# Hybrid decoder trunk: the block levels of a gated recurrence taken two at a time, in matmuls of 192 columns

## Chip, core and metric

One core of a Trainium2 chip runs the whole program. The metric is device time in microseconds (us), the median of three runs. TensorE does the matmuls (PE in the rows, its weight loads PEld), VectorE is DVE, ScalarE is ACT, GpSimd is POOL, and SyncE (SP) issues the transfers.

## What is computed

Two layers of a hybrid block on 256 tokens of width 1024, in f32. A layer is a half-step feed-forward network, a mixer of three branches (latent attention, a gated linear recurrence, attention into a memory), and a second feed-forward network. The change is in the recurrence (4 heads of 128 channels):

```python
def hgrn2_branch(q, f_logit, i_in, gate, lb, o_norm_g):
    qf = silu(q)
    g = logaddexp(log(lb), log1p(-lb) + log_sigmoid(z))     # log of the forget factor f
    k = (1.0 - lb) * sigmoid(-z)
    # S_t = diag(exp(g_t)) S_{t-1} + k_t outer v_t ; o_t = S_t^T q_t
    o = chunk_gated_recurrence(qf, k, v, g)
    return rmsnorm(o, o_norm_g) * silu(gate)
```

Written out, the output at token t is a sum over earlier tokens s of (q_t * f_{s+1} ... f_t) . k_s times v_s. The kernel forms the matrix of these products for each head and for each half of 128 tokens, and the product block of the second half with the first.

## The kernel before

Every large product is a projection: `proj` (weights as the moving operand, 512 columns), `proj_ws` and `proj_wide` (weights stationary). Weights stream from memory in chunks; ScalarE rounds each to `wh`, VectorE writes the rest to `wl` (lines 232 and 233), four buffers of each, and TensorE multiplies in three parts (lines 260 to 262). One sub-chunk is two k-tiles of 512 columns: 12 matmuls. The order of TensorE's and SyncE's work is that of the source. For VectorE and ScalarE a scheduler orders the instructions when the program is built; at run time each engine then goes through its own in that fixed order.

Small steps of the mixer are hung into the projections as jobs, run after the sub-chunk with that number: `{2: [lv(1)]}` runs `lv(1)` after the third. The recurrence uses these.

- `Tf` holds the forget factors, `Qp` and `Kp` (two halves of one tile `QKt`) hold queries and keys, channels on the partitions, tokens along the row, 4 heads of 256 tokens. `AT` collects the products of each half of 128 tokens, `A2` those across the halves.
- `diag` writes the diagonal. Then `level(s)` for s = 1, 2, 4, ..., 64 treats pairs of neighbouring blocks of s tokens: the right block's queries against all 128 keys of the half (8 matmuls of 64 columns, one for each head and half, all into one PSUM bank `hl`). VectorE copies what the mask `mk` allows into `AT` (line 752), then carries the products to the next size: right queries times the left block's factor (line 759), left keys times the right block's (line 760), and the pair's factor (line 762).
- `cross` multiplies the second half's queries with the first half's keys (4 matmuls of 128 columns into `hx`) and ScalarE copies the result to `A2`. `lv(7)` and `lv(8)` both call it.
- The jobs `lv(0)` to `lv(8)` hang in the projections ckv, hi, uk, uqn, hgate (two), gate00 (two) and gate20. Between uqn and hgate stands uqr, the projection whose result feeds the rotary step (`rope_t`, lines 850 to 856), which is VectorE's.
- The PSUM banks of the small steps rotate over four buffers (`aux`), the accumulators of the projections over two (`acc`).

Of the kernel before, what the change touches and what calls it, by code (L numbers as in the profile page):

```python
# [22 lines left out]
NT = SEQ // P  # L23
# [4 lines left out]
HH = 4  # L28
# [5 lines left out]
SK = 2  # L34
LOOKAHEAD = 3
WARM = 9
LEVELS = (1, 2, 4, 8, 16, 32)

SPLITS = (Q_LORA, KV_LORA, ROPE, 512, 512, 512, 512, 512, 3 * D)
OFF = [0]  # L40
# [104 lines left out]
def hybrid_kernel(ctx: ExitStack, tc: tile.TileContext, x, xt, mem, memt, positions, stream, smalls, ident_in, consts,  # L145
                  masks, fnorm, out):
    nc = tc.nc
# [14 lines left out]
    def T4(shape, dtype, name):  # L162
        return t4.tile(shape, dtype, tag="t4", name=name)
# [444 lines left out]
    nc.sync.dma_start(out=ident, in_=ident_in)  # L608


    mk = const.tile([P, len(LEVELS) * 64 + P], mybir.dt.uint8, name="mk")
    pos_i = const.tile([P, NT], I32, name="pos_i")
    memT = const.tile([P, KT, SEQ], F32, name="memT")
    causal = const.tile([P, P], F32, name="causal")
# [5 lines left out]
    sin2 = const.tile([P, NT, ROPE], F32, name="sin2")  # L620

    def setup_rest():
        mraw = T4([P, len(LEVELS) * 64 + P], I32, "mraw")
        nc.sync.dma_start(out=mraw, in_=masks)
        nc.vector.tensor_copy(out=mk, in_=mraw)
        nc.sync.dma_start(out=pos_i, in_=positions)
        nc.sync.dma_start(out=causal, in_=consts)
        nc.gpsimd.memset(AT, 0.0)
        raw = sm[:, LB_OFF:LB_OFF + DEPTH * HH].rearrange("p (l h) -> p l h", l=DEPTH)
        m = tiny.tile([P, HH], F32, tag="lbm", name="lbm")  # L630
        e = tiny.tile([P, DEPTH, HH], F32, tag="lbe", name="lbe")
# [57 lines left out]
    def mixer(l, u, nxt):  # L689
# [5 lines left out]


        QKt = T8([P, 2, HH, SEQ], F32, "QKt")
        Qp, Kp = QKt[:, 0], QKt[:, 1]
        Tf = T4([P, HH, SEQ], F32, "Tf")

        hf_acc = proj_ws(l, "hf", u.xb, {0: [lambda: u.bank(4)], 1: [lambda: u.bank(6)], 2: [u.finish]})
# [21 lines left out]
        def diag():  # L723
            for t in range(NT):
                b = ms_bank("hd")
                for h in range(HH):
                    nc.tensor.matmul(b[:, h * P:(h + 1) * P], lhsT=Kp[:, h, tsl[t]], rhs=Qp[:, h, tsl[t]],
                                     start=True, stop=True)
                m = mk[:, len(LEVELS) * 64:].unsqueeze(1).to_broadcast([P, HH, P])
                nc.vector.copy_predicated(out=AT[:, t], mask=m, data=b.rearrange("p (h c) -> p h c", h=HH))  # L730
            nc.vector.tensor_tensor(out=Qp, in0=Qp, in1=Tf, op=ALU.mult)

        def level(s):
            b = ms_bank("hl")
            nb = P // (2 * s)
            rows = 64 if s == 64 else P
            for t in range(NT):
                for h in range(HH):
                    i = t * HH + h
                    rhs = Qp[:, h, tsl[t]].rearrange("p (n a s) -> p n a s", a=2, s=s)[:, :, 1, :]  # L740
                    nc.tensor.matmul(b[0:rows, i * 64:(i + 1) * 64], lhsT=Kp[:, h, t * P:t * P + rows], rhs=rhs,  # L741
                                     start=True, stop=True)
            if s == 64:
                nc.vector.tensor_copy(
                    out=AT.rearrange("p t h c -> p (t h) c")[0:64, :, 64:P],
                    in_=b[0:64, :].rearrange("p (i c) -> p i c", i=NT * HH))
            else:
                i = LEVELS.index(s)
                m = mk[:, i * 64:(i + 1) * 64].rearrange("p (n s) -> p n s", s=s)
                m = m.unsqueeze(1).to_broadcast([P, NT * HH, nb, s])  # L750
                o = AT.rearrange("p t h (n a s) -> p (t h) n a s", a=2, s=s)[:, :, :, 1, :]
                nc.vector.copy_predicated(out=o, mask=m, data=b.rearrange("p (i n s) -> p i n s", i=NT * HH, s=s))
            q = Qp.rearrange("p h (n a s) -> p (h n) a s", a=2, s=s)
            k = Kp.rearrange("p h (n a s) -> p (h n) a s", a=2, s=s)
            f = Tf.rearrange("p h (n a s) -> p (h n) a s", a=2, s=s)
            n = HH * SEQ // (2 * s)
            tl = f[:, :, 0, 0:1].to_broadcast([P, n, s])
            tr = f[:, :, 1, 0:1].to_broadcast([P, n, s])
            nc.vector.tensor_tensor(out=q[:, :, 1, :], in0=q[:, :, 1, :], in1=tl, op=ALU.mult)
            nc.vector.tensor_tensor(out=k[:, :, 0, :], in0=k[:, :, 0, :], in1=tr, op=ALU.mult)  # L760
            if s < 64:
                nc.vector.tensor_tensor(out=f[:, :, 0, 0:1], in0=f[:, :, 0, 0:1], in1=f[:, :, 1, 0:1], op=ALU.mult)

        def cross():
            b = ms_bank("hx")
# [2 lines left out]
            nc.scalar.copy(out=A2, in_=b.rearrange("p (h c) -> p h c", h=HH))  # L768

        def lv(i):  # L770
            if i < len(LEVELS):
                return lambda: level(LEVELS[i])
            return (lambda: level(64)) if i == len(LEVELS) else cross


        accs = proj_u("cq", {3: [diag]})
# [252 lines left out]
        def gate(b, h, jobs=None):  # L1029
            accs = proj_u(f"gate{b}{h}", jobs)  # L1030
            g = T4([P, NT, 512], F32, f"gate{b}")
            for t in range(NT):
                nc.scalar.activation(out=g[:, t, :], in_=accs[t], func=AF.Copy if h == 0 else AF.Sigmoid,
                                     scale=u.r[:, t:t + 1])
            gts[(b, h)] = g
# [37 lines left out]
        for t in range(NT):  # L1073
            nc.scalar.activation(out=hg["gate"][:, t, :], in_=accs[t], func=AF.Silu, scale=u.r[:, t:t + 1])
        gate(0, 0, {0: [qk_T(ksb, kT, 1), lv(6)], 1: [qk_T(qsb, qT, 1)], 2: [att(0), lv(7)], 3: [att(1)]})
        gate(2, 0, {0: [att(2), lv(8)], 1: [ptr(0)], 2: [ptr(1), att(3)], 3: [app(0)]})
        gate(1, 0, {0: [app(1), ptr(2), att(4)], 1: [ptr(3), hg_out], 2: [app(2), att(5)], 3: [app(3), ptr(4)]})
        mem_T("qmT", "mq", u.xb, [{3: [open_gates, mem_split], 7: [app(4), ptr(5)]}, {3: [hg_T], 7: [app(5)]}])
        mem_T("kmT", "mk", mem_xb, [{}, {}])
# [67 lines left out]
def _consts():  # L1147
    q, k = np.meshgrid(np.arange(P), np.arange(P), indexing="ij")
    c = np.where(k > q, np.float32(NEG), np.float32(0.0)).astype(np.float32)
    m = np.zeros((P, len(LEVELS) * 64 + P), np.int32)  # L1150
    s = np.arange(P)
    for i, h in enumerate(LEVELS):
        t = np.array([t for t in range(P) if (t // h) % 2 == 1])
        m[:, i * 64:(i + 1) * 64] = ((s[:, None] // (2 * h)) == (t[None, :] // (2 * h))) & \
            (((s[:, None] // h) % 2) == 0)
    m[:, len(LEVELS) * 64:] = np.eye(P, dtype=np.int32)
    return c, m


# [26 lines left out]
```

## Time and profile before

| | |
|---|---|
| median of 3 runs | 1304.21 us (1304.02 to 1305.16) |
| the profiled execution's own time | 1304.3 us, its span 1302.5 us |
| mean granted TensorE clock | 0.997 of full speed |
| TensorE busy | 1290.9 us, 99% of the span |
| VectorE busy | 920.4 us, 71% |
| ScalarE busy | 734.3 us, 56% |

The span is the time between the first and the last instruction; the program's time has 1.8 us more around it. Busy times are averages over the whole program. An engine's queue is strictly in order, so a busy share tells nothing of where one of its results comes too late for another engine; that is read from the order and the starts of the instructions. Both layers run the same mixer, the second 642.7 us after the first.

### The profile page before, as it was taken

The page shows a single profiled execution, that of the slowest core. Times are in us where ns is not written, and L with a number is a line of the kernel's source. Part 1 is how long each engine was busy: PE and PEld are TensorE (multiplying, and loading weights), DVE is VectorE, ACT ScalarE, POOL GpSimd, SP SyncE. Part 2 cuts the span into 40 slices and gives each one's busy share as a digit, 9 for nine tenths or more (in the row PEclk, how much of TensorE's full clock was granted, in tenths as well). Part 3 has the DMA queues.
Part 4 walks back from the last instruction along what each step waited for, and adds up shares of the span by engine and source line. Part 5 has one row for each costly group of instructions (what it writes and reads, how often), then busy time and mean ns, then how long its engine had stood idle before and what let it go on. Part 6 is the DMA issues. An engine that isn't in the chain of part 4 may idle for free.

```text
span 1302.5 us, 18358 instructions
## 1 busy us (share of the span) xinstructions
PE 1290.9 (99%) x7139; PEld 1118.1 (86%) x7139; DVE 920.4 (71%) x1433; ACT 734.3 (56%) x1139; POOL 4.6 (0%) x18
## 2 busy tenths in 40 slices
PE   9999999999999999999999999999999999999997
PEld 7888889888888898888898888898888888988885
DVE  6987557777876677775577775577688756777753
ACT  6765446547765465554455554465477644655542
POOL 1000000000000000000000000000000000000000
PEclk9999999999999999999999999999999999999998
DMA  8755554433444545555545555445334455555561
GB/s 292 281 187 191 196 192 150 166 133 128 155 168 162 194 164 192 194 193 180 194 177 194 194 183 189 173 154 171 126 130 162 162 183 176 190 184 183 188 220 51
DMA packets 35801, 231.28 MB, mean 178 GB/s; under 512 B 4225, under 2 KB 4609, under 8 KB 10369
## 3 DMA queue, kind: packets, MB, share of 16 engines
q1 hardware_dynamic: 35568, 230.05, 50.7%
q8 instruction: 56, 0.92, 0.3%
q14 instruction: 33, 0.26, 0.1%
q10 hardware_dynamic: 144, 0.05, 0.0%
HBM read 229.04 MB, written 1.05 MB: 177 GB/s over the span
## 4 chain that ended last, share of the span: by engine, by line
PE 99%; DVE 0%; DMA 0%; ACT 0%; SPq 0%; issue 0%
PE acc L321 26%; PE acc L260 15%; PE acc L262 15%; PE acc L261 15%; PE acc L326 13%; PE hl L741 2%; PE acc L305 2%; PE acc L303 2%; PE acc L301 2%; PE sc L884 1%; PE pt L587 1%; PE nt L404 1%; PE po L901 1%; PE at L587 1%; PE mo L901 0%; PE msc L970 0%
## 5 line engine op out<-in xcount | busy, mean ns | idle before, releaser
L233 DVE TENSOR_TENSOR wl<-raw,wh 128x1024 fp32r<-128x1024 f32 (+2 forms) x435 | 523.6, 1205 | 290.4 <-ACT wh L232 282.9
L232 ACT CAST wh<-raw 128x1024 fp32r<-128x1024 f32 (+2 forms) x435 | 449.3, 1034 | 428.9 <-PE acc L261 271.0
L321 PE MATMUL acc<-nT,wh 128*128 128x512 f32 x1408 | 443.7, 397 | 0.0
L326 PEld LDWEIGHTS acc<-nT,wl 128*128 128x128 f32 x1408 | 264.8, 188 | 62.1
L326 PE MATMUL acc<-nT,wl 128*128 128x256 f32 x1408 | 277.0, 278 | 0.0
L321 PEld LDWEIGHTS acc<-nT,wh 128*128 128x128 f32 x1408 | 214.4, 189 | 0.0
L260 PE MATMUL acc<-wh,hTh 128*128 128x512 f32 x352 | 137.8, 391 | 0.0
L262 PE MATMUL acc<-wl,hTh 128*128 128x512 f32 x352 | 137.3, 390 | 0.0
L261 PE MATMUL acc<-wh,hTl 128*128 128x512 f32 x352 | 137.2, 390 | 0.0
L260 PE MATMUL acc<-wh,nT 128*128 128x512 f32 (+2 forms) x320 | 125.0, 391 | 0.0
L262 PE MATMUL acc<-wl,nT 128*128 128x512 f32 (+2 forms) x320 | 120.5, 377 | 0.0
L261 PE MATMUL acc<-wh,nT 128*128 128x512 f32 (+2 forms) x320 | 120.2, 376 | 0.0
L374 ACT CAST hTh<-jn 128x256 fp32r<-128x256 f32 x80 | 32.4, 406 | 94.9 <-DVE jn L484 94.9
L262 PEld LDWEIGHTS acc<-wl,hTh 128*128 128x128 f32 x352 | 66.1, 188 | 13.8
L260 PEld LDWEIGHTS acc<-wh,hTh 128*128 128x128 f32 x352 | 66.1, 188 | 13.4
L261 PEld LDWEIGHTS acc<-wh,hTl 128*128 128x128 f32 x352 | 66.2, 188 | 13.4
L262 PEld LDWEIGHTS acc<-wl,nT 128*128 128x128 f32 x320 | 60.1, 188 | 10.6
L260 PEld LDWEIGHTS acc<-wh,nT 128*128 128x128 f32 x320 | 60.3, 188 | 8.9 <-ACT qsb L841 0.3
L261 PEld LDWEIGHTS acc<-wh,nT 128*128 128x128 f32 x320 | 60.4, 189 | 8.6
L336 DVE TENSOR_TENSOR jn<-acc,jn 128x512 f32<-128x512 f32 x92 | 62.9, 683 | 0.2
L375 DVE TENSOR_TENSOR hTl<-jn,hTh 128x256 fp32r<-128x256 f32 x80 | 33.9, 424 | 33.6 <-ACT hTh L374 33.6
L301 PE MATMUL acc<-nT,wh 128*128 128x256 f32 x192 | 55.6, 289 | 0.2 <-ACT wh L232 0.2
(295 smaller groups left out, 1583.9 us busy)
## 6 DMA issues: line engine op xcount, KB each, us to landing
raw<-in_stream SPq DMA_DIRECT2D x197, 1024.0 KB, 4.8
raw<-in_stream SPq DMA_DIRECT2D x17, 512.0 KB, 3.6
raw<-in_stream SPq DMA_DIRECT2D x6, 768.0 KB, 4.4
raw<-in_stream SPq DMA_DIRECT2D x4, 576.0 KB, 3.7
x<-in_x SPq DMA_DIRECT2D x4, 256.0 KB, 6.0
memT<-in_memt SPq DMA_DIRECT2D x1, 1024.0 KB, 7.1
mrow<-in_mem SPq DMA_DIRECT2D x2, 512.0 KB, 9.1
out_x<-xg SPq DMA_DIRECT2D x4, 256.0 KB, 2.4
```

The source lines that it names most:

```text
L232: last_wh[0] = nc.scalar.copy(out=wh, in_=raw[:, a:a + m, :])
L233: nc.vector.tensor_tensor(out=wl, in0=raw[:, a:a + m, :], in1=wh.bitcast(F32), op=ALU.subtract)
L260: nc.tensor.matmul(o, lhsT=xh(k)[:, ts], rhs=wh[:, j, :], start=(k == 0), stop=False)
L261: nc.tensor.matmul(o, lhsT=xl(k)[:, ts], rhs=wh[:, j, :], start=False, stop=False)
L262: nc.tensor.matmul(o, lhsT=xh(k)[:, ts], rhs=wl[:, j, :], start=False, stop=(k == nkt - 1))
L301: nc.tensor.matmul(o, lhsT=wh[:, j, fs], rhs=x[:, 0, :], start=first, stop=False, skip_group_check=True)
L303: nc.tensor.matmul(o, lhsT=wh[:, j, fs], rhs=x[:, 1, :], start=False, stop=False, skip_group_check=True)
L321: nc.tensor.matmul(a2[:, f].rearrange("p a c -> p (a c)"), lhsT=wh[:, j, fs], rhs=x.rearrange("p a c -> p (a c)"), start=(k == 0), stop=False,
L326: nc.tensor.matmul(a2[:, f, 0, :], lhsT=wl[:, j, fs], rhs=x[:, 0, :], start=False, stop=(k == KT - 1), skip_group_check=True)
L336: last_join[1] = nc.vector.tensor_tensor(out=s, in0=a2[:, :, 0, :], in1=s, op=ALU.add)
L374: nc.scalar.copy(out=oh, in_=ps)
L375: nc.vector.tensor_tensor(out=ol, in0=ps, in1=oh.bitcast(F32), op=ALU.subtract)
```

## The change

Levels are taken in pairs: `four(i, t)` treats groups of four neighbouring blocks of s = 1, 4 or 16 tokens, for half t. Each group of four holds the pairs of two levels, and what was a level of its own (a block against the one before, two before and three before) comes from one matmul of 192 columns: 96 from `Qp` (blocks 1 to 3) and 96 from a second copy `Qs`, in which blocks 2 and 3 carry one factor more and block 3 two more. `Qs` takes the place of `Kp` in the tile `QKt`; `Kp` gets its own tile. A call makes 4 matmuls into two banks, and six masked copies of 192, 128 and 64 elements. `Qs` is made on VectorE in the call for t = 0; queries, keys and factors are carried on in the call for t = 1. There are six calls, and they stand in the slots of the six levels from 1 to 32. Level 64 stays as it was, and the second `cross` is gone. The mask input grows from 512 to 704 columns.

```diff
-LEVELS = (1, 2, 4, 8, 16, 32)
+LEVELS = (1, 4, 16)
+MCOLS = len(LEVELS) * 192
...
-        Qp, Kp = QKt[:, 0], QKt[:, 1]
+        Qp, Qs = QKt[:, 0], QKt[:, 1]
+        Kp = T4([P, HH, SEQ], F32, "Kp")
...
-        def level(s):
+        def four(i, t):
+            s = LEVELS[i]
+            hn = HH * SEQ // (4 * s)
+            q, z, k, f = (a.rearrange("p h (n b s) -> p (h n) b s", b=4, s=s) for a in (Qp, Qs, Kp, Tf))
+
+            def fb(a, n=1, to=None):
+                return f[:, :, a:a + n, 0:1].to_broadcast([P, hn, to or n, s])
+
+            if t == 0:
+                nc.vector.tensor_tensor(out=z[:, :, 1:3, :], in0=q[:, :, 2:4, :], in1=fb(1, 2), op=ALU.mult)
+                nc.vector.tensor_tensor(out=z[:, :, 3:4, :], in0=z[:, :, 2:3, :], in1=fb(1), op=ALU.mult)
+            for h0 in (0, 2):
+                b = ms_bank("hl")
+                for h in (h0, h0 + 1):
+                    rhs = QKt[:, :, h, tsl[t]].rearrange("p a (n c) -> p a n c", c=4 * s)[:, :, :, s:4 * s]
+                    nc.tensor.matmul(b[:, (h - h0) * 192:(h - h0 + 1) * 192], lhsT=Kp[:, h, tsl[t]], rhs=rhs,
+                                     start=True, stop=True)
+                d = b[:, 0:384].rearrange("p (h a n c) -> p h a n c", h=2, a=2, c=3 * s)
+                o = AT[:, t, h0:h0 + 2].rearrange("p h (n c) -> p h n c", c=4 * s)
+                m0 = i * 192
+                for a, lo, hi in ((0, s, 4 * s), (1, 2 * s, 4 * s), (2, 3 * s, 4 * s)):
+                    w = hi - lo
+                    nq = w * P // (4 * s)
+                    m = mk[:, m0:m0 + nq].rearrange("p (n c) -> p n c", c=w)
+                    m0 += nq
+                    src = d[:, :, 0] if a == 0 else d[:, :, 1, :, 0:w] if a == 1 else d[:, :, 1, :, 2 * s:3 * s]
+                    nc.vector.copy_predicated(out=o[:, :, :, lo:hi],
+                                              mask=m.unsqueeze(1).to_broadcast([P, 2, P // (4 * s), w]), data=src)
+            if t == 1:
+                nc.vector.tensor_tensor(out=q[:, :, 1:2, :], in0=q[:, :, 1:2, :], in1=fb(0), op=ALU.mult)
+                nc.vector.tensor_tensor(out=q[:, :, 2:4, :], in0=z[:, :, 1:4:2, :], in1=fb(0, 1, 2), op=ALU.mult)
+                for a in (2, 1):
+                    nc.vector.tensor_tensor(out=f[:, :, a, 0:1], in0=f[:, :, a, 0:1], in1=f[:, :, a + 1, 0:1],
+                                            op=ALU.mult)
+                nc.vector.tensor_tensor(out=k[:, :, 0:3, :], in0=k[:, :, 0:3, :], in1=fb(1, 3), op=ALU.mult)
+                nc.vector.tensor_tensor(out=f[:, :, 0, 0:1], in0=f[:, :, 0, 0:1], in1=f[:, :, 1, 0:1], op=ALU.mult)
...
-            if i < len(LEVELS):
-                return lambda: level(LEVELS[i])
-            return (lambda: level(64)) if i == len(LEVELS) else cross
+            if i < 2 * len(LEVELS):
+                return lambda: four(i // 2, i % 2)
+            return level64 if i == 2 * len(LEVELS) else cross
...
-        gate(2, 0, {0: [att(2), lv(8)], 1: [ptr(0)], 2: [ptr(1), att(3)], 3: [app(0)]})
+        gate(2, 0, {0: [att(2)], 1: [ptr(0)], 2: [ptr(1), att(3)], 3: [app(0)]})
```

How the built order changes, at the two places of which the prediction speaks. The first is VectorE around the third group (s = 16). Before, after the copy and the carries of the level of 8 tokens (the 752 to 762 rows), come the weight remainders and the rotary step; the next level's matmuls need only what stands in the first four rows.

```order
L752 COPY_PREDICATED AT<-mk,hl 128x64x8
L759 TENSOR_TENSOR QKt<-QKt,Tf 128x64x8
L760 TENSOR_TENSOR QKt<-QKt,Tf 128x64x8
L762 TENSOR_TENSOR Tf<-Tf 128x64
L233 TENSOR_TENSOR wl<-raw,wh 128x1024 x2
L850 TENSOR_TENSOR rope_t<-rope_t,cos_166 128x288
L853 TENSOR_TENSOR rope_t<-rope_t,sin_167 128x9x16 x2
...
L856 COPY ksb<-rope_t 128x8x32
L853 TENSOR_TENSOR rope_t<-rope_t,sin_167 128x9x16
L233 TENSOR_TENSOR wl<-raw,wh 128x1024
L854 TENSOR_TENSOR qsb<-rope_t 128x8x32
```

Now (one line further down in the source, so 234 for 233 and 876 to 882 for the rotary step) the carries of the second group are 764 to 770, and the two products that make the third group's `Qs`, lines 744 and 745, stand behind the rotary step. They are written into `QKt`.

```order
L764 TENSOR_TENSOR QKt<-QKt,Tf 128x64x4
...
L769 TENSOR_TENSOR Kp<-Kp,Tf 128x64x12
L770 TENSOR_TENSOR Tf<-Tf 128x64
L234 TENSOR_TENSOR wl<-raw,wh 128x1024 x2
L876 TENSOR_TENSOR rope_t<-rope_t,cos_166 128x288
L879 TENSOR_TENSOR rope_t<-rope_t,sin_167 128x9x16 x2
...
L234 TENSOR_TENSOR wl<-raw,wh 128x1024
L880 TENSOR_TENSOR qsb<-rope_t 128x8x32
L881 TENSOR_TENSOR rope_t<-rope_t 128x32
L744 TENSOR_TENSOR QKt<-QKt,Tf 128x16x32
L882 COPY ksb<-rope_t 128x8x32
L745 TENSOR_TENSOR QKt<-QKt,Tf 128x16x16
```

What moved: the operands of the next matmuls are no longer complete before the rotary step but after it. The first of the four 192-column matmuls of `four(2, 0)` waits for line 745.

The second place is VectorE between the call for the first group's second half and the second group, a stretch that had two masked copies and six products and now reads:

```order
L761 COPY_PREDICATED AT<-mk,hl 128x64x3
L234 TENSOR_TENSOR wl<-raw,wh 128x1024
L761 COPY_PREDICATED AT<-mk,hl 128x64x2
L761 COPY_PREDICATED AT<-mk,hl 128x64x3
L761 COPY_PREDICATED AT<-mk,hl 128x64
L761 COPY_PREDICATED AT<-mk,hl 128x64x2
...
L765 TENSOR_TENSOR QKt<-QKt,Tf 128x256x2
L769 TENSOR_TENSOR Kp<-Kp,Tf 128x256x3
L770 TENSOR_TENSOR Tf<-Tf 128x256
L234 TENSOR_TENSOR wl<-raw,wh 128x512
L744 TENSOR_TENSOR QKt<-QKt,Tf 128x64x8
L745 TENSOR_TENSOR QKt<-QKt,Tf 128x64x4
```

What moved: carries for four blocks and the new `Qs` all stand between two calls that follow each other on TensorE. TensorE's own order is unchanged but for the calls themselves; the call for the third group stands after hgate's first sub-chunk, where the level of 16 tokens stood:

```order
L261 MATMUL acc<-wh,nT 128x512
L262 MATMUL acc<-wh,nT 128x512
L263 MATMUL acc<-wl,nT 128x512
L750 MATMUL hl<-QKt,Kp 128x192 x4
L261 MATMUL acc<-wh,nT 128x512
```

What moved: eight matmuls of 64 columns became four of 192 in the same place.

## Rows read from the trace of the kernel before

**Rows 1.** The page's busy times by engine.

```profile
PE 1290.9 (99%) x7139; PEld 1118.1 (86%) x7139; DVE 920.4 (71%) x1433; ACT 734.3 (56%) x1139; POOL 4.6 (0%) x18
```

**Rows 2.** Waits of TensorE, the longest: releaser, us in total, times, longest.

```profile
PE warm L198 <- DVE eps_t L546: 1.2, 1, 1.2
```

**Rows 3.** Timeline of TensorE, first layer: start us, us, form; x16 are 8 matmuls.

```profile
247.20 0.48 PE L260 MATMUL acc<-wh,nT 128*128 128x512 f32 x1
...
252.77 1.89 PE L741 MATMUL hl<-QKt 128*128 128x64 f32 x16
...
260.01 1.89 PE L741 MATMUL hl<-QKt 128*128 128x64 f32 x16
261.71 0.48 PE L260 MATMUL acc<-wh,cqT 128*128 128x512 f32 x1
...
263.19 0.28 PE L260 MATMUL acc<-wh,cqT 128*128 128x256 f32 x1
...
265.46 0.50 PE L260 MATMUL acc<-wh,nT 128*128 128x512 f32 x1
...
268.34 1.89 PE L741 MATMUL hl<-QKt 128*128 128x64 f32 x16
...
301.40 1.03 PE L884 MATMUL sc<-kT,qT 96*128 96x256 f32 x4
302.27 1.06 PE L767 MATMUL hx<-QKt 128*128 128x128 f32 x8
303.08 0.47 PE L260 MATMUL acc<-wh,nT 128*128 128x512 f32 x1
```

**Rows 4.** Timeline of VectorE, first layer, levels of 2 and 4 tokens.

```profile
247.83 1.31 DVE L752 COPY_PREDICATED AT<-mk,hl 128x512 f32<-128x512 uint8 x1
248.93 0.22 DVE L348 TENSOR_TENSOR lr_a<-lr_y 128x4 f32<-128x4 f32 x1
...
250.32 0.64 DVE L762 TENSOR_TENSOR Tf<-Tf 128x256 f32<-128x256 f32 x1
250.87 0.68 DVE L233 TENSOR_TENSOR wl<-raw,wh 128x512 fp32r<-128x512 f32 x1
...
254.70 0.71 DVE L752 COPY_PREDICATED AT<-mk,hl 128x512 f32<-128x512 uint8 x1
255.31 0.68 DVE L759 TENSOR_TENSOR QKt<-QKt,Tf 128x512 f32<-128x512 f32 x1
```

**Rows 5.** Timeline of VectorE from the level of 8 tokens to that of 16.

```profile
262.26 0.74 DVE L370 SCALAR_TENSOR_TENSOR vml<-acc,lr_y,vml 128x512 fp32r<-128x512 f32 x1
262.92 0.71 DVE L752 COPY_PREDICATED AT<-mk,hl 128x512 f32<-128x512 uint8 x1
...
264.90 1.22 DVE L233 TENSOR_TENSOR wl<-raw,wh 128x1024 fp32r<-128x1024 f32 x1
...
267.69 0.45 DVE L850 TENSOR_TENSOR rope_t<-rope_t,cos 128x288 f32<-128x288 f32 x1
...
269.95 1.21 DVE L233 TENSOR_TENSOR wl<-raw,wh 128x1024 fp32r<-128x1024 f32 x1
271.08 0.41 DVE L854 TENSOR_TENSOR qsb<-rope_t 128x256 f32<-128x256 f32 x1
...
271.52 0.71 DVE L752 COPY_PREDICATED AT<-mk,hl 128x512 f32<-128x512 uint8 x1
```

**Rows 6.** Windows at the end; after the DVE, ACT and POOL sums come PEclk, DMA share, GB/s.

```profile
1293.00:1294.00 1.00, 0.40 (x2) 0.00 (x0) 0.56 (x1) 0.00 (x0) 0.00 (x0) 1.00 0.00 0
1295.00:1296.00 1.00, 0.00 (x0) 0.00 (x0) 1.00 (x3) 0.88 (x3) 0.00 (x0) 0.74 0.02 8
1296.00:1297.00 1.00, 0.00 (x0) 0.00 (x0) 0.93 (x10) 0.43 (x2) 0.00 (x0) 0.50 0.00 0
```

**Rows 7.** Timeline of TensorE at the start.

```profile
1.19 4.02 PE L198 MATMUL warm<-wz 128*128 128x512 bf16 x9 [1.19 <-DVE eps_t L546]
...
7.41 1.47 PE L198 MATMUL warm<-wz 128*128 128x512 bf16 x6
```

More of the change, by code (lines that the diff above doesn't have):

```diff
@@ L608, in hybrid_kernel @@
     nc.sync.dma_start(out=ident, in_=ident_in)
-    mk = const.tile([P, len(LEVELS) * 64 + P], mybir.dt.uint8, name="mk")
+    mk = const.tile([P, MCOLS + P], mybir.dt.uint8, name="mk")
     pos_i = const.tile([P, NT], I32, name="pos_i")
@@ L622, in setup_rest @@
     def setup_rest():
-        mraw = T4([P, len(LEVELS) * 64 + P], I32, "mraw")
+        mraw = T4([P, MCOLS + P], I32, "mraw")
         nc.sync.dma_start(out=mraw, in_=masks)
@@ L728, in diag @@
                                      start=True, stop=True)
-                m = mk[:, len(LEVELS) * 64:].unsqueeze(1).to_broadcast([P, HH, P])
+                m = mk[:, MCOLS:].unsqueeze(1).to_broadcast([P, HH, P])
                 nc.vector.copy_predicated(out=AT[:, t], mask=m, data=b.rearrange("p (h c) -> p h c", h=HH))
             nc.vector.tensor_tensor(out=Qp, in0=Qp, in1=Tf, op=ALU.mult)
-        def level(s):
+        def four(i, t):
[32 more added lines that the diff above has]
+                nc.vector.tensor_tensor(out=f[:, :, 0, 0:1], in0=f[:, :, 0, 0:1], in1=f[:, :, 1, 0:1], op=ALU.mult)
@@ L734, in level, with level64 @@
+        def level64():
             b = ms_bank("hl")
-            nb = P // (2 * s)
-            rows = 64 if s == 64 else P
             for t in range(NT):
@@ L739, in level @@
                     i = t * HH + h
-                    rhs = Qp[:, h, tsl[t]].rearrange("p (n a s) -> p n a s", a=2, s=s)[:, :, 1, :]
-                    nc.tensor.matmul(b[0:rows, i * 64:(i + 1) * 64], lhsT=Kp[:, h, t * P:t * P + rows], rhs=rhs,
+                    rhs = Qp[:, h, t * P + 64:(t + 1) * P]
+                    nc.tensor.matmul(b[0:64, i * 64:(i + 1) * 64], lhsT=Kp[:, h, t * P:t * P + 64], rhs=rhs,
                                      start=True, stop=True)
[L743 to L758, printed above, removed]
+            nc.vector.tensor_copy(
+                out=AT.rearrange("p t h c -> p (t h) c")[0:64, :, 64:P],
+                in_=b[0:64, :].rearrange("p (i c) -> p i c", i=NT * HH))
+            q, k, f = (a.rearrange("p h (n a s) -> p (h n) a s", a=2, s=64) for a in (Qp, Kp, Tf))
+            n = HH * NT
+            tl = f[:, :, 0, 0:1].to_broadcast([P, n, 64])
+            tr = f[:, :, 1, 0:1].to_broadcast([P, n, 64])
             nc.vector.tensor_tensor(out=q[:, :, 1, :], in0=q[:, :, 1, :], in1=tl, op=ALU.mult)
             nc.vector.tensor_tensor(out=k[:, :, 0, :], in0=k[:, :, 0, :], in1=tr, op=ALU.mult)
-            if s < 64:
-                nc.vector.tensor_tensor(out=f[:, :, 0, 0:1], in0=f[:, :, 0, 0:1], in1=f[:, :, 1, 0:1], op=ALU.mult)
         def cross():
@@ L1149, in _consts @@
     c = np.where(k > q, np.float32(NEG), np.float32(0.0)).astype(np.float32)
-    m = np.zeros((P, len(LEVELS) * 64 + P), np.int32)
+    m = np.zeros((P, MCOLS + P), np.int32)
     s = np.arange(P)
[L1152 to L1156, printed above, removed]
+    c0 = 0
+    for h in LEVELS:
+        b = (s // h) % 4
+        for gap in (1, 2, 3):
+            t = s[b >= gap]
+            m[:, c0:c0 + t.size] = ((s[:, None] // (4 * h)) == (t[None, :] // (4 * h))) & (b[:, None] == b[None, t] - gap)
+            c0 += t.size
+    m[:, MCOLS:] = np.eye(P, dtype=np.int32)
     return c, m
```

## The prediction

> **What bounds the kernel now.** I read the page's busy times first. TensorE is busy for 1290.9 of 1302.5 us [rows 1], so with a granted clock near full the time is the sum of TensorE's work plus whatever makes it wait. The list of TensorE's waits comes next: the longest in the whole program is 1.2 us, at the start [rows 2]. Nothing in the mixers makes TensorE wait, and two things follow. Every matmul taken away shortens the program by its own length, in either layer. And every microsecond by which a new order makes TensorE wait for VectorE or ScalarE lengthens it at full price, since there is no idle time to soak it up. VectorE is busy 71% on the mean [rows 1]; that tells nothing of whether one of its results comes too late, so the third view is the timeline of TensorE beside that of VectorE in the stretch of the recurrence, 245 to 304 us in the first layer [rows 3 to 5]. The second layer is the same stretch 642.7 us later, and the built order of the change is the same in both, so everything below is worked out once and doubled.
>
> **What the change takes off TensorE.** One level of 64-column matmuls goes from 260.01 to 261.71, which is 1.70 us for 16 instructions (each f32 matmul is issued as two), so 106 ns each [rows 3]. Four instructions of 256 columns, the `sc` row at 301.40, take 0.87 us to the next start at 302.27, so 217 ns each [rows 3]. A 256-column instruction costs two 64-column ones and not four, so at 64 columns the columns are not what sets the pace. By columns from the 256-column row, 192 columns cost 217 x 192/256 = 163 ns. A call has 4 matmuls, 8 instructions: 1.30 us in place of 1.70. Six calls: -2.4 us for each layer. The second `cross` ran from 302.27 to 303.08: -0.8 us [rows 3]. Together -3.2 us for each layer, -6.4 in all. Its copy on ScalarE goes too, which TensorE never waited for.
>
> What could spoil this is the way `rhs` is read: for s = 1 three of every four elements, in two pieces. Nothing in the trace shows such a read at 192 columns. The bounds: 163 ns, or, if the 106 ns of the 64-column row were all the reading of its 64 strided columns, 106 x 3 = 318 ns, and a call would be 2.5 us. I take 163, because the 64-column rows are alike for all strides, 1.89 us at each level [rows 3], which points to a cost outside the read.
>
> **What the change adds on VectorE.** Durations here are from start to next start, since instructions overlap by about 0.1 us. A masked copy of 512 elements takes 0.61 us at blocks of 4 tokens (254.70 to 255.31) but 1.10 at blocks of 2 (247.83 to 248.93); a product of 256 elements that lie four apart takes 0.55 (250.32 to 250.87) [rows 4], and a product of 512 elements takes 0.6. With about 0.07 us of fixed cost this is 1 ns an element at runs of 4 or more, and twice that for copies in short runs and for products of lone elements. So the three copies of one bank (192, 128, 64 elements) cost 0.27 + 0.20 + 0.14 = 0.61 us at s = 4 and 16 and 0.47 + 0.34 + 0.20 = 1.01 at s = 1; both banks twice that. `Qs` costs 0.60 + 0.33 (0.62 + 0.55 at s = 1), the carries of queries 0.33 + 0.60 (0.55 + 0.62), of keys 0.87 (768 elements), a factor 0.2 (0.55). For runs of 3 and 2 there is one rule to weigh. The copies in pairs cost double in the row above. The Trainium skill, SBUF — State Buffer, under the section on the DMA port swizzle, says that two or more accesses to a 16-byte line run at full rate; by it the first group's copies would cost 0.61 a bank and the first of the waits below would be 0.8 us shorter. The row contradicts it for these copies, so I go by the row.
>
> This work is off TensorE's path so long as its results come in time. Weight remainders have room: the one written at 250.87 is first used when the second sub-chunk of uqn starts, 261.71 [rows 4, 3]. The results that have little room are `Qs`, keys and queries for the next call. So I follow VectorE's queue from call to call, in the built order.
>
> **Second group, s = 4.** Let T be the start of `four(0, 1)` on TensorE. The next call is due after 1.30 us for the call and 5.57 us of projection (247.20 to 252.77 [rows 3]): T + 6.9. VectorE can begin at T + 0.7, when the first bank is done, and has to get through: one copy 0.47, a remainder 1.14 (269.95 to 271.08 [rows 5]), the other five copies 1.55, queries 1.17, keys 0.87, factor 0.55, a remainder of 512 columns 0.6, `Qs` 0.60 + 0.33. That is 7.3, so T + 8.0, and 0.1 for the hand-over. TensorE waits 1.2 us; if only the 3-element runs go at full rate, 0.8. I take 1.0.
>
> **Third group, s = 16.** Let T be the start of `four(1, 1)`. TensorE's work until the next call: the call 1.30, the rest of uqn 1.48 (261.71 to 263.19), uqr 2.27 (to 265.46), hgate's first sub-chunk 2.88 (to 268.34) [rows 3]. VectorE from T + 0.7: one copy 0.27, a remainder 1.14, `vml` 0.66 (262.26 to 262.92 [rows 5]). uqr needs the accumulator that `vml` frees, so it starts at T + 2.95 and not at 2.78: a wait of 0.2. The next call is therefore due at T + 8.1. VectorE goes on: the last copies and carries 2.93 (0.20 + 0.27 + 0.14 + 0.20 + 0.33 + 0.14 + 0.60 + 0.87 + 0.18), two remainders 2.28, the rotary step 2.26 (267.69 to 269.95), a remainder 1.13, the end of the first rotary half 0.44 (271.08 to 271.52) [rows 5], and only now `Qs`: 0.60, a copy of keys 0.20, 0.33. That reaches T + 13.0, with the hand-over T + 13.1. TensorE waits 5.0 us. Before, the same queue reached 271.52 as late as T + 11.5 counted from the level at 260.01, and nobody noticed: the level at 268.34 needed only what was written before the remainder at 264.90, T + 4.9 [rows 5]. The change puts the operands on the other side of the rotary step. What is queued behind the waiting matmul is the rest of hgate, so everything after it shifts, and none of it is given back. Past this point VectorE has caught up: the next calls need nothing that it has not some microseconds for.
>
> **The clock.** TensorE would stand idle for 5 us. In this trace it was idle as long only once, at the end: its last matmul ends at about 1293.4, and the granted clock is 1.00 until 1295, 0.74 in the next microsecond and 0.50, the lower of its two levels, from 1296 [rows 6]. So after some 2 us of idleness it fell. What it costs to come back the start shows: 9 matmuls of 512 columns take 4.02 us from rest, 447 ns each, while a little later 6 take 1.47, 245 each [rows 7]; the loss is 4.02 - 9 x 0.245 = 1.8 us. For a wait of 5 us the cost is between 0 and 1.8 us; I take 1.5, near the start's, since the wait is more than twice what it took to fall.
>
> **The sum.** For each layer -2.4 - 0.8 + 1.0 + 0.2 + 5.0 + 1.5 = +4.5 us, in all +9.0. The larger mask adds 0.2 us of VectorE's time in the first feed-forward network, under TensorE's projections. The profiled execution took 1304.3 us (1302.5 of span), the median of the runs is 0.1 less: 1313.
>
> **Rivals.**
> Stalls without the clock. The long wait may be shorter than the clock needs: +3.0 a layer, 1310.3. For it, waits under 1 us at the start cost nothing of the kind; against it, the end.
> Faster. VectorE's lag is smaller than I make it, and the third group's `Qs` is there in time. All of the gain then stands: 1304.3 - 6.4 = 1297.9. The place is the wait for line 745 before the third group; with the 1.2 us of the other waits it decides at 2.0 us: shorter, and the change gains. For it, VectorE is 71% busy [rows 1]. Against it, from T + 0.7 on the queue has no gap in my sum, and its pieces are rows of this very stretch; they would have to be 3 us too long in 12.
> Strided reads. If 192 strided columns cost 318 ns, each call costs 1.2 us more: +7.2 a layer, 1327; at s = 1 alone 1318. Against it, that stride makes no difference at 64 columns.
>
> **How the numbers follow.** Waits and clock: 0.50. Waits alone: 0.30. Faster: 0.11. Strided reads: 0.06. The remaining 0.03 is a long wait near its point of decision, no change. One measurement of this kernel tells 0.2%, 2.6 us, from no change. The waits' bounds (4.4 to 5.6 for the long one, 0.8 to 1.3, the clock 0 to 1.8) give +1.9 to +5.9 a layer, 1308 to 1316; the range goes a little beyond, 1306 to 1317, and leaves out the faster case and the strided one. Slower 0.86, same 0.03, faster 0.11.
>
> **What would show it.** A row of waits of TensorE's line 750 for VectorE's line 745, four times in all, near 1 us and near 5 us; uqr waiting some 0.2 us; a granted clock of 0.50 in the microseconds after the longer ones; rows of the calls at 1.3 us, alike for s = 1, 4 and 16. Wrong would be: no wait on line 745, or one under 2 us at the third group, or calls of 2.5 us.

## The result, and the profile after

The changed kernel takes 1316.52 us, the median of 5 runs (1314.95 to 1316.81), against 1304.23 us (1304.02 to 1305.16) for the kernel before: a ratio of 1.0088, with an interval from 1.0077 to 1.0099. It is slower by 12.3 us. The profiled execution took 1315.39 us, with a span of 1313.6 us, 11.1 us longer than the span before; the other four spans lie between 1313.2 and 1315.0. Its mean granted clock is 0.993, before 0.997.

The page's busy times come first; they answer to [rows 1].

```profile
PE 1289.0 (98%) x7027; PEld 1113.7 (85%) x7027; DVE 932.6 (71%) x1505; ACT 733.6 (56%) x1137; POOL 4.6 (0%) x18
```

TensorE has 112 instructions fewer and is busy for 1.9 us less, not the 6.4 us less that the removed matmuls were to give, while the span is 11.1 us longer. So the new time is idle (13.0 us more), and some work also became slower. The list of TensorE's waits (what waits, on what; us in total, times, longest) says where the idle time is. The longest wait of before was the one on `eps_t` [rows 2].

```profile
PE hl L750 <- DVE QKt L745: 12.7, 4, 5.0
PE warm L199 <- DVE eps_t L547: 1.2, 1, 1.2
PE acc L306 <- DVE wl L234: 1.0, 2, 0.6
PE acc L261 <- DVE vml L371: 0.4, 2, 0.2
```

The waits for `eps_t` and for `wl` stand at the program's start, and the kernel before has them too (1.2 us each). All of the new waits but 0.4 us are for one line, the second product of `Qs`. The timeline of TensorE shows them in the first layer, in brackets at the end of a row: before the second group 1.33 us, at uqr 0.22, before the third group 4.99. It answers to [rows 3].

```profile
244.81 1.46 PE L750 MATMUL hl<-QKt,Kp 128*128 128x192 f32 x8
...
253.06 1.54 PE L750 MATMUL hl<-QKt,Kp 128*128 128x192 f32 x8 [1.33 <-DVE QKt L745]
...
259.91 1.46 PE L750 MATMUL hl<-QKt,Kp 128*128 128x192 f32 x8
261.07 0.53 PE L261 MATMUL acc<-wh,cqT 128*128 128x512 f32 x1
...
262.96 0.39 PE L261 MATMUL acc<-wh,cqT 128*128 128x256 f32 x1 [0.22 <-DVE vml L371]
...
273.12 2.93 PE L750 MATMUL hl<-QKt,Kp 128*128 128x192 f32 x8 [4.99 <-DVE QKt L745]
275.60 0.88 PE L261 MATMUL acc<-wh,nT 128*128 128x512 f32 x1
...
278.26 0.40 PE L261 MATMUL acc<-wh,nT 128*128 128x512 f32 x1
...
283.24 1.47 PE L750 MATMUL hl<-QKt,Kp 128*128 128x192 f32 x8
284.41 0.52 PE L261 MATMUL acc<-wh,nT 128*128 128x512 f32 x1
...
285.93 0.40 PE L261 MATMUL acc<-wh,nT 128*128 128x512 f32 x1
```

The call at 273.12 needs 2.48 us to the next start (275.60); the same call at 283.24 needs 1.17. The call and the six matmuls behind it take 5.14 us (273.12 to 278.26) after the long wait and 2.69 (283.24 to 285.93) without it: 2.45 us lost to the clock, besides the wait. The windows show the clock itself (the columns are those of [rows 6]).

```profile
268.00:270.00 2.00, 0.13 (x1) 0.00 (x0) 2.00 (x9) 1.03 (x1) 0.00 (x0) 1.00 0.29 57
270.00:272.00 2.00, 0.00 (x0) 0.00 (x0) 2.00 (x6) 0.00 (x0) 0.00 (x0) 0.81 1.03 430
272.00:274.00 2.00, 0.88 (x3) 0.88 (x4) 1.35 (x5) 0.00 (x0) 0.00 (x0) 0.50 0.09 37
...
276.00:278.00 2.00, 2.00 (x7) 1.54 (x6) 0.90 (x3) 0.00 (x0) 0.00 (x0) 0.50 0.00 0
278.00:280.00 2.00, 2.00 (x10) 1.66 (x9) 0.00 (x0) 0.38 (x1) 0.00 (x0) 0.98 0.00 0
```

TensorE falls idle at 268.13. A mean of 0.81 over the second window is 1.24 us at 1.00 and the rest at 0.50, so the clock fell to the lower of its two levels at about 271.2, 3.1 us into the wait. It is back at 278.1, 5.0 us after TensorE resumed. VectorE is busy all through the first four microseconds (the third sum in a row, 2.00 of 2.00): it is not waiting for anything itself, it is doing other work first. Its timeline says which; it answers to [rows 4, 5].

```profile
245.87 0.44 DVE L761 COPY_PREDICATED AT<-mk,hl 128x192 f32<-128x192 uint8 x1
246.17 1.21 DVE L234 TENSOR_TENSOR wl<-raw,wh 128x1024 fp32r<-128x1024 f32 x1
247.29 1.31 DVE L761 COPY_PREDICATED AT<-mk,hl 128x128 f32<-128x128 uint8 x4
248.39 0.66 DVE L764 TENSOR_TENSOR QKt<-QKt,Tf 128x256 f32<-128x256 f32 x1
248.90 0.45 DVE L761 COPY_PREDICATED AT<-mk,hl 128x64 f32<-128x64 uint8 x1
249.03 0.84 DVE L765 TENSOR_TENSOR QKt<-QKt,Tf 128x512 f32<-128x512 f32 x1
...
252.49 0.42 DVE L745 TENSOR_TENSOR QKt<-QKt,Tf 128x256 f32<-128x256 f32 x1
...
265.75 2.36 DVE L234 TENSOR_TENSOR wl<-raw,wh 128x1024 fp32r<-128x1024 f32 x2
268.02 0.46 DVE L876 TENSOR_TENSOR rope_t<-rope_t,cos 128x288 f32<-128x288 f32 x1
...
270.27 1.22 DVE L234 TENSOR_TENSOR wl<-raw,wh 128x1024 fp32r<-128x1024 f32 x1
271.40 0.42 DVE L880 TENSOR_TENSOR qsb<-rope_t 128x256 f32<-128x256 f32 x1
...
271.84 0.69 DVE L744 TENSOR_TENSOR QKt<-QKt,Tf 128x512 f32<-128x512 f32 x1
...
272.65 0.42 DVE L745 TENSOR_TENSOR QKt<-QKt,Tf 128x256 f32<-128x256 f32 x1
...
285.16 1.28 DVE L761 COPY_PREDICATED AT<-mk,hl 128x192 f32<-128x192 uint8 x6
286.35 0.42 DVE L764 TENSOR_TENSOR QKt<-QKt,Tf 128x256 f32<-128x256 f32 x1
```

From 265.75 to 271.84 VectorE makes weight remainders and the rotary step, and then the two products that TensorE has been waiting for since 268.13. The last two rows are the six copies of the third group's second half, for comparison further down. The second layer repeats this: waits of 1.34, 0.22 and 4.99 us, and a clock that falls 3.4 us after TensorE's last matmul and comes back 5.2 us after it resumes.

### The profile page after: what moved, and what is told of

Same layout as the page of the kernel before. It is cut to its first block, busy times and chain, and to the rows that moved or that the text cites. A ratio compares the mean times of both kernels' runs of the same rounds, so it can differ in the third digit from the quotient of the medians.

```text
span 1313.6 us, 18211 instructions
## 1 busy us (share of the span) xinstructions
PE 1289.0 (98%) x7027; PEld 1113.7 (85%) x7027; DVE 932.6 (71%) x1505; ACT 733.6 (56%) x1137; POOL 4.6 (0%) x18
## 4 chain that ended last, share of the span: by engine, by line
PE 95%; DVE 3%; DMA 0%; issue 0%; ACT 0%; SPq 0%; DVEq 0%
PE acc L322 26%; PE acc L261 15%; PE acc L262 14%; PE acc L263 14%; PE acc L327 13%; PE acc L306 2%; PE acc L304 2%; PE acc L302 2%; DVE wl L234 1%; PE hl L750 1%; PE sc L910 1%; PE pt L588 1%; PE nt L405 1%; PE po L927 1%; PE at L588 1%; DMA xT<-in_xt 0%
## 5 line engine op out<-in xcount | busy, mean ns | idle before, releaser
L327 PE MATMUL acc<-nT,wl 128*128 128x256 f32 x1408 | 276.7, 278 | 0.0
L306 PE MATMUL acc<-nT,wl 128*128 128x256 f32 x192 | 54.7, 285 | 1.1 <-DVE wl L234 1.0
```

What stands on the lines that cost most here:

```text
L306: nc.tensor.matmul(o, lhsT=wl[:, j, fs], rhs=x[:, 0, :], start=False, stop=(k == nkt - 1), skip_group_check=True)
L327: nc.tensor.matmul(a2[:, f, 0, :], lhsT=wl[:, j, fs], rhs=x[:, 0, :], start=False, stop=(k == KT - 1), skip_group_check=True)
```

## The experiments

The theory behind the prediction, called ORDER below: `Qs` of the next group is made too late because of where it stands in VectorE's queue, and the long idle time lets the clock fall. Its rival, LOAD: VectorE simply has too much work in this stretch, with the longer masked copies and carries, and TensorE would wait wherever `Qs` stands. The first four kernels share their runs of the kernel before (median 1304.34 us of 19 runs), the last four theirs (1304.30 us of 12).

**`Qs` ahead of the rotary step.** The next group's `Qs` is made at the end of the call before it; the work is the same.

```diff
-            if t == 0:
-                nc.vector.tensor_tensor(out=z[:, :, 1:3, :], in0=q[:, :, 2:4, :], in1=fb(1, 2), op=ALU.mult)
-                nc.vector.tensor_tensor(out=z[:, :, 3:4, :], in0=z[:, :, 2:3, :], in1=fb(1), op=ALU.mult)
+            if i == 0 and t == 0:
+                second(0)
...
                 nc.vector.tensor_tensor(out=f[:, :, 0, 0:1], in0=f[:, :, 0, 0:1], in1=f[:, :, 1, 0:1], op=ALU.mult)
+                if i + 1 < len(LEVELS):
+                    second(i + 1)
```

> Qs of the next group is made at the end of the call for the second half, so on VectorE it stands ahead of the rotary step. Theory ORDER (the third group's matmuls wait because Qs stands behind the rotary step, and the clock falls because TensorE is idle for 5 us): Qs is complete about 9.1 us after the start of the call before, against 8.2 when it is due, so the wait of 4.99 us shrinks to about 0.9 in each layer, the granted clock stays 1.00, the 1.33 us wait of the second group stays, and the span of 1313.6 loses 2 x (4.1 + 2.5) = 13 us: about 1300.5. Rival LOAD (VectorE has too much to do in this stretch, wherever Qs stands): TensorE waits about as long in some other place, 1311 to 1314.

Measured: 1302.88 us (1302.66 to 1303.59, 10 runs), ratio 0.9989 (0.998 to 0.9999), span 1300.8, mean clock 0.998. The call for the third group in TensorE's timeline of this kernel:

```profile
269.20 1.57 PE L758 MATMUL hl<-QKt,Kp 128*128 128x192 f32 x8 [0.97 <-DVE QKt L742]
```

and VectorE's timeline ahead of it:

```profile
267.00 0.68 DVE L741 TENSOR_TENSOR QKt<-QKt,Tf 128x512 f32<-128x512 f32 x1
267.60 1.21 DVE L234 TENSOR_TENSOR wl<-raw,wh 128x1024 fp32r<-128x1024 f32 x1
268.73 0.41 DVE L742 TENSOR_TENSOR QKt<-QKt,Tf 128x256 f32<-128x256 f32 x1
269.07 0.45 DVE L886 TENSOR_TENSOR rope_t<-rope_t,cos 128x288 f32<-128x288 f32 x1
```

The two products now stand ahead of the rotary step, the wait is 0.97 us in place of 4.99, and 13.6 us are gone from the time with no work taken out. That speaks for ORDER: the same load on VectorE, in another order, costs 0.97 us here in place of 4.99 and the slow clock behind it. The 0.97 us that are left have a weight remainder of 1.13 us (267.60) between the two products. The wait before the second group stays at 1.3 us, and the time is no better than that of the kernel before without its second `cross` (1302.66 us, below): the two waits still take all that the calls gain.

**The removed `cross` by itself.** The kernel before, without the second computation of the products across chunks, and otherwise as it was.

```diff
-        gate(2, 0, {0: [att(2), lv(8)], 1: [ptr(0)], 2: [ptr(1), att(3)], 3: [app(0)]})
+        gate(2, 0, {0: [att(2)], 1: [ptr(0)], 2: [ptr(1), att(3)], 3: [app(0)]})
```

> The kernel before without its second cross, nothing else. ORDER: 0.8 us less in each layer, span 1300.9. Rival (this work was hidden anyway): 1302.5.

Measured: 1302.66 us (1302.43 to 1303.16, 10 runs), ratio 0.9987 (0.9978 to 0.9997): 1.68 us, 0.84 for each layer. The term of 0.8 stands.

**The long wait filled with other matmuls.** The changed kernel, with five f32 matmuls of 512 columns into a bank that nothing reads, just ahead of the call for the third group. The wait for `Qs` has the same end; TensorE is at work through most of it.

```diff
+        def fill(n):
+            b = ms_bank("fill")
+            for _ in range(n):
+                nc.tensor.matmul(b, lhsT=ident, rhs=memT[:, 0:2, :].rearrange("p k c -> p (k c)"),
+                                 start=True, stop=True)
...
-        accs = proj_u("hgate", {0: [lv(4)], 2: [qk_T(ksb, kT, 0), lv(5)], 3: [qk_T(qsb, qT, 0)]})
+        accs = proj_u("hgate", {0: [lambda: fill(5), lv(4)], 2: [qk_T(ksb, kT, 0), lv(5)], 3: [qk_T(qsb, qT, 0)]})
```

> The changed kernel, with 5 f32 matmuls of 512 columns into a bank that nobody reads ahead of the third group's call, so that TensorE works for about 4.3 us of the 5 us that it waits. ORDER: the wait on VectorE shrinks to about 0.7 us, Qs comes at the same time, the granted clock stays 1.00, and the call takes 1.2 us in place of 2.5: 2.5 us less in each layer, span about 1308.6. Rival (the slow rows behind the wait have another cause than the idle time): the rows stay slow and the span 1313.6 or more.

Measured: 1311.06 us (1310.72 to 1312.08, 4 runs), ratio 1.0052 (1.0035 to 1.0069), span 1309.5, mean clock 0.998. The timeline of TensorE in this kernel:

```profile
268.67 4.45 PE L775 MATMUL fill<-memT,ident 128*128 128x512 f32 x10
273.83 1.57 PE L750 MATMUL hl<-QKt,Kp 128*128 128x192 f32 x8 [0.70 <-DVE QKt L745]
275.10 0.52 PE L261 MATMUL acc<-wh,nT 128*128 128x512 f32 x1
```

The call starts as late as in the changed kernel (in this execution the recurrence runs some 0.7 us later from its start on: its second call is at 245.53, not 244.81), but it and the matmul behind it run at full speed: 1.27 us to the next start in place of 2.48. Added matmuls made the kernel 5.5 us faster. The lower clock is therefore a cost of its own: 2.45 us a layer by the rows above, 2.7 by the medians, 2.1 by the spans, or 2.4 once the later start of the recurrence is allowed for.

**The second group's wait.** The changed kernel, with the six masked copies of the call ahead of the second group left out.

```diff
-                for a, lo, hi in ((0, s, 4 * s), (1, 2 * s, 4 * s), (2, 3 * s, 4 * s)):
+                for a, lo, hi in ((0, s, 4 * s), (1, 2 * s, 4 * s), (2, 3 * s, 4 * s))[:0 if (i, t) == (0, 1) else 3]:
```

> The changed kernel without the six masked copies of the first group's second half; these products are missing from AT. ORDER: VectorE has 1.5 us less to do between the two calls, the second group's wait of 1.33 us vanishes, the third group's stays at 5.0: span 1310.9. Rival (that wait hangs on the weight remainders in between, which wait for ScalarE): it stays at 1 us or more, span 1313.

Measured: 1312.05 us (1311.12 to 1312.32, 4 runs), ratio 1.0057 (1.0042 to 1.0072). From the list of TensorE's waits of this kernel:

```profile
PE hl L750 <- DVE QKt L745: 10.0, 2, 5.0
```

from TensorE's timeline, the call ahead of the second group's:

```profile
245.01 1.46 PE L750 MATMUL hl<-QKt,Kp 128*128 128x192 f32 x8
```

and from VectorE's timeline, the end of the second group's `Qs`:

```profile
251.10 0.42 DVE L745 TENSOR_TENSOR QKt<-QKt,Tf 128x256 f32<-128x256 f32 x1
```

TensorE waits for line 745 twice and not four times. Counted from the call before, line 745 starts at 6.09 us (251.10 less 245.01) and not at 7.68 (252.49 less 244.81): 1.59 us less on VectorE took the wait of 1.33 away. So this wait, the smaller one, yields to less work on VectorE, as LOAD has it. Whether another order of the same work would do as much, no run tried: two weight remainders, 1.72 us together (at 246.17 and 251.17), stand in the same stretch ahead of `Qs`. The long wait is untouched at 5.0 us. The time fell by 4.5 us by the medians and by 3.1 by the spans, where two waits of 1.33 are 2.7; the rest is not explained.

This execution also shows where the clock falls in two more waits of 5 us (columns as in [rows 6]):

```profile
270.00:272.00 2.00, 0.24 (x1) 0.24 (x2) 1.97 (x8) 0.00 (x0) 0.00 (x0) 0.73 0.35 147
...
276.00:278.00 2.00, 2.00 (x6) 1.57 (x6) 0.00 (x0) 0.00 (x0) 0.00 (x0) 0.56 0.00 0
...
916.00:918.00 2.00, 0.00 (x0) 0.00 (x0) 2.00 (x5) 0.00 (x0) 0.00 (x0) 0.51 0.99 418
...
922.00:924.00 2.00, 2.00 (x8) 1.60 (x7) 0.78 (x3) 0.00 (x0) 0.00 (x0) 0.78 0.00 0
```

In the first layer the clock fell at 270.9, 4.2 us after TensorE's last matmul; in the second at 916.0, 2.1 us after it. The last section takes this up.

**The third group's call later.** The changed kernel, with the calls for the third group behind hgate's third and fourth sub-chunks instead of the first and third. `Qs` stays behind the rotary step.

```diff
-        accs = proj_u("hgate", {0: [lv(4)], 2: [qk_T(ksb, kT, 0), lv(5)], 3: [qk_T(qsb, qT, 0)]})
+        accs = proj_u("hgate", {2: [qk_T(ksb, kT, 0), lv(4)], 3: [qk_T(qsb, qT, 0), lv(5)]})
```

> The changed kernel with the third group's two calls hung after hgate's third and fourth sub-chunk, in place of the first and third. Qs is still made behind the rotary step. ORDER (a wait for a result that is late by a fixed time): the call is due 5.5 to 6.5 us later, Qs comes about 1 us later than before since one more remainder stands ahead of it, so the wait of 4.99 us is gone, the clock stays 1.00 and the 1.33 us wait of the second group remains: span 1298.6. Rival LOAD (VectorE is short of time in this stretch): TensorE waits at the fourth sub-chunk or at level 64 in its place, 1303 or more.

Measured: 1300.84 us (1300.57 to 1301.68, 8 runs), ratio 0.9974 (0.9963 to 0.9984), span of the profiled execution 1299.7. Waits on line 745 are left only before the second group (2.7 us in two). This is 1.1 us above the expected span, but 1.0 of it was there before the mixers: the transposition at their start comes at 242.39 here and at 241.40 in the profiled execution of the changed kernel. This execution waited 2.6 us at its first weights, that one 1.0, at a place that the edit does not touch. The median run has a span of 1299.1.

**Both groups later.** The same, and the second group's first call behind uv's first sub-chunk instead of uk's.

```diff
-        accs = proj(l, "uk", ckv_h, ckv_l, {0: [lv(2)]})
+        accs = proj(l, "uk", ckv_h, ckv_l)
...
-        accs = proj(l, "uv", ckv_h, ckv_l)
+        accs = proj(l, "uv", ckv_h, ckv_l, {0: [lv(2)]})
```

> As e5, and the second group's first call hung into uv in place of uk, one sub-chunk (2.7 us) later. ORDER: no wait on line 745 is left, span 1313.6 - 2 x (4.99 + 2.5 + 1.33) = 1296.0, which is the whole gain of the matmuls and of the cross. Rival: the copies of that call now stand in front of vml, and uqr waits for vml by more than 0.2 us: 1297 to 1299.

Measured: 1298.05 us (1297.96 to 1298.47, 5 runs), ratio 0.9953 (0.9939 to 0.9966), span 1296.2. All of TensorE's waits of this kernel:

```profile
PE warm L199 <- DVE eps_t L547: 1.2, 1, 1.2
PE acc L261 <- DVE vml L371: 0.4, 2, 0.2
```

Every instruction of the changed kernel is there, VectorE is as busy (931.2 us against 932.6), and the time is 18.5 us shorter. Against the kernel before without its second `cross` it is 4.6 us faster; with the 0.4 us of the wait at uqr this is 5.05 us for 12 calls, 0.42 a call.

**`Qs` early and both groups later.** The edit of the first experiment, the second group in uv, and the third group's first call behind hgate's second sub-chunk, one earlier than in the two kernels above.

```diff
-        accs = proj_u("hgate", {0: [lv(4)], 2: [qk_T(ksb, kT, 0), lv(5)], 3: [qk_T(qsb, qT, 0)]})
+        accs = proj_u("hgate", {1: [lv(4)], 2: [qk_T(ksb, kT, 0), lv(5)], 3: [qk_T(qsb, qT, 0)]})
```

> Qs of the next group early as in e1, the third group's first call one sub-chunk later (after hgate's second), the second group's first call in uv. ORDER: the two waits that e1 kept, 1.3 and 0.97 us, are gone, span 1300.8 - 2 x 2.3 = 1296.2, the same as e6 within 1 us. Rival: the second call of the third group waits for its banks, because the first one's copies stand behind the rotary step: 1297 to 1300.

Measured: 1297.68 us (1296.77 to 1297.93, 5 runs), ratio 0.9948 (0.9935 to 0.996), span 1295.9, with no wait on `Qs`. It is the fastest of all and beats the kernel before as well as the changed one. Its lead over the one above is 0.4 us: the two sets of five runs only just do not overlap, the intervals of the ratios do, so the lead is not to be built on.

**The long wait filled in part.** As the filled wait above, with three matmuls in place of five, to see at what wait the clock falls.

```diff
-        accs = proj_u("hgate", {0: [lambda: fill(5), lv(4)], 2: [qk_T(ksb, kT, 0), lv(5)], 3: [qk_T(qsb, qT, 0)]})
+        accs = proj_u("hgate", {0: [lambda: fill(3), lv(4)], 2: [qk_T(ksb, kT, 0), lv(5)], 3: [qk_T(qsb, qT, 0)]})
```

> As e3 with 3 matmuls in place of 5: TensorE is idle for about 2.4 us ahead of the third group's call in place of 0.7. If the fall of the clock needs the 3 us or more of idleness that preceded it in the changed kernel: 1.00 throughout and the span of e3, 1309.5. If 2 us are enough, as at the end of the program: the call again takes about 2.5 us, 1313 to 1314.

Measured: 1311.98 us (1310.83 to 1312.76, 4 runs), ratio 1.0058 (1.0044 to 1.0071). Neither expectation holds for both layers. The timeline of TensorE in the first layer and in the second:

```profile
273.69 1.73 PE L750 MATMUL hl<-QKt,Kp 128*128 128x192 f32 x8 [2.42 <-DVE QKt L745]
274.96 0.88 PE L261 MATMUL acc<-wh,nT 128*128 128x512 f32 x1
...
921.23 1.57 PE L750 MATMUL hl<-QKt,Kp 128*128 128x192 f32 x8 [2.43 <-DVE QKt L745]
```

and the windows behind them:

```profile
274.00:276.00 2.00, 2.00 (x10) 1.89 (x9) 1.21 (x5) 0.00 (x0) 0.00 (x0) 0.74 0.03 8
276.00:278.00 2.00, 2.00 (x6) 1.56 (x5) 0.39 (x2) 0.00 (x0) 0.00 (x0) 0.50 0.00 0
...
922.00:924.00 2.00, 2.00 (x11) 1.76 (x11) 1.56 (x6) 0.00 (x0) 0.00 (x0) 1.00 0.00 0
```

Two waits of the same length, 2.42 and 2.43 us, in one execution: after the first the clock fell, at about 275.0, when TensorE had been at work again for 1.3 us, and was back at 278.4; after the second it did not fall. What decides between the two stays open.

## Why the prediction was right

The forecast was 1313 us, in a range from 1306 to 1317, and slower. It measured 1316.5, by the mechanism that was given, and near the upper end of the range. Term by term, for each layer, in us:

| term | forecast | measured | from |
|---|---|---|---|
| six calls of 192 columns | -2.4 | -2.5 | both groups later, against before without the second cross |
| second `cross` left out | -0.8 | -0.84 | that edit alone |
| wait before the second group | +1.0 | +1.33 | timeline of after |
| wait at uqr | +0.2 | +0.22 | timeline of after |
| wait before the third group | +5.0 | +4.99 | timeline of after |
| clock after the long wait | +1.5 | +2.45 | timeline of after |
| sum | +4.5 | +5.65 | |

Twice 5.65 is 11.3 us; the spans differ by 11.1 and the medians by 12.3. Part of the last microsecond lies ahead of the recurrence: the transposition at the first mixer's start came at 242.10 in the profiled execution before and at 241.40 in the one after, so that from there on the change costs 11.8 us. The rest is of the size by which executions of one kernel differ (1313.2 to 1315.0 in span), and stays unexplained.

That 1316.5 lies inside the range is in part luck. The bounds named beside it add up to +2.2 to +5.7 us a layer (not +1.9 to +5.9), 1308.7 to 1315.7; the measured time is 0.8 us beyond them, because the clock cost more than its bound, and falls into the margin that was put on top.

**The calls.** A call takes 1.16 us to the next start (259.91 to 261.07), a little less than the 1.30 scaled down from 256 columns, but the matmul behind it takes 0.37 to its next start, where the one behind a level of 64 columns took 0.32; by these rows a call saves 0.49 us, by whole runs 0.42. Whether strided reads cost something is settled: the calls at s = 1 (1.16 and 1.17 us), s = 4 (1.16) and s = 16 (1.17) are alike, and that rival falls.

**The long wait** came out as worked out, end by end: `Qs` was to be done at T + 13.0 and was at T + 13.1 (272.98 with T at 259.91), the call was due at T + 8.1 and was at T + 8.2. Summing VectorE's queue from its own rows, in the built order, gave a wait within 0.1 us, and its pieces agree one by one (the last copies and carries 2.93 us in both, from 262.82 to 265.75). That the cause is the order and not the load, the first experiment shows: same work, 4 us less wait.

**The second wait** I worked out at 1.2 us and took at 1.0, since I allowed for short runs of 3 elements at full rate. Here it goes the other way: two of my pieces were wrong in opposite directions. The six copies took 0.30 + 1.10 + 0.13 = 1.53 us to next starts, not 2.02; but VectorE was free only at T + 1.06 (245.87, with T at 244.81), not at T + 0.7, since it still had small products to do (lines 349 to 371) that I had not counted. The same six copies in runs of 16 and more, at s = 16, took 1.19 us (285.16 to 286.35), 0.60 a bank; the prediction had 0.61 for long runs.

The Trainium skill (SBUF — State Buffer, the section on the DMA port swizzle) states that two accesses to a 16-byte line are enough for full rate. Copies of single elements have one access to a line, so the 0.61 a bank that the prediction worked out by this rule leaves out their share; with the prediction's 0.20 for them the rule gives an estimate of 0.67. At 0.77 a bank the measured copies lie between that and the 1.01 that I went by, nearer the rule. At 0.67 a bank the wait would have been 1.1 us, an estimate as well.

None of this moves the result. This wait yields to less work on VectorE, as the kernel without the copies shows; there LOAD holds as far as it was tested.

**The clock** is the step that was mis-sized: I put its price at 1.5 us with 1.8 as its upper bound, taken from the nine matmuls at the program's start [rows 7]. That the clock falls in a wait of 5 us was right, and the filled wait shows that this cost is apart from the wait. But it stayed low for 5.0 us after TensorE resumed, and cost 2.45. The bound was no bound: a start-up was taken as the most that a return can cost, when it was only one instance of it, and not even a fixed one. In the execution of the kernel with both groups later the six matmuls that took 1.47 us in [rows 7] took 2.12, so that the start cost more than the 1.8 read there:

```profile
8.49 2.12 PE L199 MATMUL warm<-wz 128*128 128x512 bf16 x6
```

With 2.45 in its place the sum would have been +5.45 a layer, 1315.2 us. The rival of waits without the clock falls with the granted clock of 0.50 behind both long waits.

**The gain** was not lost in the matmuls, as the rival of strided reads would have it: with both groups' calls later, the time is 1298.05 us, close to the 1297.9 that I gave for the case in which `Qs` comes in time. The waits, and the clock that fell in the long ones, cost more than it.

## What to carry to other kernels

When a change makes an operation cheaper on the engine that sets the end but gives its operands more steps, write down the other engine's queue in the built order from the moment its input appears, and add its rows up to the due time: sums of rows of this kernel gave a 5 us wait to 0.1 us, which no share of busy time (71% before and after) hints at. A wait on TensorE of several microseconds can be dearer than its length, here by about half: filling it, even with work that nobody needs, gave back 5.5 of the 12.3 us. If the operands cannot be earlier, the consumer can be later: three of six calls moved behind more of the independent projections turned a loss of 12.3 us into a gain of 6.3.

## What the runs showed of the hardware that was not expected

The granted clock fell at no fixed time in a wait. Five falls lie behind waits of the third group; the times are read from TensorE's rows and from the windows' clock, in us:

| execution and layer | wait | fall, after the last matmul | back, after TensorE resumed | low for | loss |
|---|---|---|---|---|---|
| changed kernel, first | 4.99 | 3.1 | 5.0 | 6.8 | 2.4 |
| changed kernel, second | 4.99 | 3.4 | 5.2 | 6.8 | 2.5 |
| without the copies, first | 5.00 | 4.2 | 6.0 | 6.8 | 2.8 |
| without the copies, second | 4.99 | 2.1 | 4.0 | 6.8 | 1.9 |
| filled in part, first | 2.42 | 3.7 | 4.7 | 3.4 | 1.6 |

The loss is the time from the third group's first call to the transposition behind hgate's third sub-chunk, less the 6.89 us that this takes in both layers of the filled kernel, where the clock stayed at 1.00. The four waits of 5 us had the clock low for the same 6.8 us, and the later it fell the more of that lay behind the wait, where TensorE had work to do and lost time. So the clock behind a wait of 5 us cost between 1.9 and 2.8 us here, and 2.45 is one value out of that. TensorE was busy all the while until the clock was back. At the program's end it fell some 2 us after the last matmul [rows 6].

With a wait of 2.4 us the fall was not certain: one of two such waits in one execution had it, and there the clock fell when TensorE was at work again, so that a wait already over still slowed the projections behind it. Waits of up to 1.34 us never had it in these traces.

The six masked copies in runs of 3, 2 and 1 elements took 1.53 us for 768 elements. With the prediction's fixed 0.07 us for each taken off, that is 1.4 ns an element, where the level in runs of two took 2.0 (1.10 us for 512) and the one in runs of four 1.1 (0.61 us) [rows 4]. That the length of the runs matters, and not the size of the copies, the same six copies at s = 16 show: in runs of 48, 32 and 16 elements they took 1.19 us, 1.0 ns an element.
